# The last head pair's norm is taken up during the attention, through a buffer in DRAM, and its new sample state is formed among its value projections

## The chip, the cores and the metric

The kernel runs on one core of a Trainium2 chip. The metric is device time in microseconds (us) of one execution. The core has five engines, each with its own queue that it works through in order: PE (TensorE, matmuls), DVE (VectorE), ACT (ScalarE), POOL (GpSimd) and SP (SyncE, which issues nearly all DMAs). They wait for each other by semaphores.

## The reference

One inference step of one decoder layer: 1024 prompt tokens and 8 x 4 sample tokens, model width 1024. Two branches read the same normalised input: sparse attention (8 heads, 2 key heads, the 256 best keys of an indexer) and retention (8 heads of 64). What the change touches is the retention and its merge:

```python
def _head_norm(o):
    mu = jnp.mean(o, axis=-1, keepdims=True)
    var = jnp.mean(jnp.square(o - mu), axis=-1, keepdims=True)
    return (o - mu) * lax.rsqrt(var + EPS)

def step(S, inp):                       # in _retention, over chunks of 128
    qc, kc, vc = inp
    inter = jnp.einsum('bchk,bhkv->bchv', qc * dec_in[None, :, :, None], S)
    scores = jnp.einsum('bchk,bshk->bhcs', qc, kc) * dmat[None]
    intra = jnp.einsum('bhcs,bshv->bchv', scores, vc)
    S = S * dec_chunk[None, :, None, None] + jnp.einsum('bchk,bchv->bhkv', kc * dec_out[None, :, :, None], vc)
    return S, inter + intra
...
yb = jax.nn.silu(gb) * _head_norm(ob).reshape(B, T, D_B).astype(x.dtype)
y = jnp.einsum('bte,ed->btd', jnp.concatenate([ya, yb], axis=-1), w_out)
```

The retention also returns its final state for the prompt and, for the sample tokens, the state that starts from a given one (`state_ret`).

## The kernel before

The kernel goes through stages: input norm, scores of the indexer, bisections that find each row's 256th best score, the retention in four pairs of heads (0 to 3), the sparse attention in eight query blocks, the output projection with its norm, and the gated embedding. A scheduler orders the instructions of each engine ahead of time by a simulated timeline; at run time each engine keeps that order. Tiles of a pool with the same tag share buffers (`bufs`), and a new tile waits until the one whose buffer it takes has been read for the last time, also by a DMA that stores it.

**The retention** (L1440 to L1513). For each pair there is a query-and-key phase and a value phase. Each has eight blocks of 128 tokens, 24 matmuls of 128 x 256 each (`mm_a`, lines L276 to L278; results `pqk` and `pvg`), and one product for the sample rows (`mm_s`). In the query-and-key phase DVE and POOL rotate each block (`rope`). In the value phase ACT takes the values and the gates out of `pvg` (`take_vg`: values scaled into `vv`, gates by Silu into `sg`, ten buffers), `chunk_mm` forms the scores of the block, and the sum of the block goes from PSUM to `acc[:, tb, :]` by ACT (L1502). After the eighth block `ret_sample` does the same for the sample rows: outputs against the given states `s0`, and then the new state (`vm` on DVE, `dst` on PE, `sso` on DVE, store to `ret_state_sample`). Then `norm_gate` runs twice, for the eight prompt blocks (16 columns of statistics) and for the sample rows (2 columns): statistics and coefficients gy and gz on DVE with a root on ACT, scaling of `acc` on ACT (L1117) and DVE (L1119), product with the gates on POOL, for pair 3 on DVE (L1122), and a store to `yb_d` in DRAM (L1123). Between the blocks, `steps` moves generators on by a step: `bp` (prompt bisection) and `bss` (sample bisection, with a conditional part whose branch is at L976) in pair 0, `ss` (the sample attention's selection, mostly DVE) in pairs 1 to 3. What is left of `bss` is issued at the start of pair 1 with high priority, but an engine comes to the branch only where its order has it.

**The attention** (L1551 to L1635). At its start SP loads `toep` (1 MB) for the position bias. For each query block and each of two key heads (kv): `near` from `toep` and the mask on DVE, scores `sa` on PE, `L` with its row minimum `mn` on DVE (L1602), exponentials on ACT (L1605), transposes `ptp` and products `ob` on PE. Query blocks (`qas`) and gates (`gat`) come by SP's loads, two buffers each. Beside this the generator `sa` runs the sample attention: gathers on POOL (`kvs`, `kw`, L1170) and its own matmuls. The output projection then reads `yb_d`.

## Time and profile before

| | us |
|---|---|
| median of three runs | 1051.2 (1048.44 to 1052.79) |
| the profiled execution | 1050.72 |
| its span | 1048.9 |
| mean granted PE clock | 0.976 |
| pair 1: query-and-key phase, value phase start | 400.05, 433.35 |
| pair 2: query-and-key phase, value phase start | 471.03, 505.19 |
| pair 3: query-and-key phase, value phase start | 549.38, 586.84 |
| end of pair 3's last value projection | 623.0 |
| first load of the output projection | 790.78 |

The starts are those of the first 128 x 256 matmul of a phase in the timeline. Times in profile rows are us from the start of the span, durations of one instruction in ns where the row says "mean ns". PEclk is the share of the full clock that the throttle granted.

### The profile page before, as it was taken

The page shows a single profiled execution, that of the slowest core. Times are in us where ns is not written, and L with a number is a line of the kernel's source. Part 1 is how long each engine was busy: PE and PEld are TensorE (multiplying, and loading weights), DVE is VectorE, ACT ScalarE, POOL GpSimd, SP SyncE. Part 2 cuts the span into 40 slices and gives each one's busy share as a digit, 9 for nine tenths or more (in the row PEclk, how much of TensorE's full clock was granted, in tenths as well). Part 3 has the DMA queues.
Part 4 walks back from the last instruction along what each step waited for, and adds up shares of the span by engine and source line. Part 5 has one row for each costly group of instructions (what it writes and reads, how often), then busy time and mean ns, then how long its engine had stood idle before and what let it go on. Part 6 is the DMA issues. An engine that isn't in the chain of part 4 may idle for free.

```text
span 1048.9 us, 19845 instructions
## 1 busy us (share of the span) xinstructions
PE 991.8 (95%) x7375; PEld 838.2 (80%) x7375; DVE 681.4 (65%) x2022; ACT 503.1 (48%) x1090; POOL 320.8 (31%) x425
## 2 busy tenths in 40 slices
PE   4999998999999899999899995999999999999998
PEld 3999997766776898889788783666666999999998
DVE  6847668898492657969949937787763423873332
ACT  5545565885434487612342335656545523442211
POOL 4203223121301522705803512634330522332200
PEclk9999999999999999999899995999999999999999
DMA  8211235545443311311210724533211312432211
GB/s 291 71 61 51 96 97 190 186 148 177 130 161 115 76 33 43 81 45 47 64 54 21 190 65 128 162 78 109 73 56 48 118 42 81 148 116 87 83 41 38
DMA packets 98310, 102.25 MB, mean 97 GB/s; under 512 B 21346, under 2 KB 88386, under 8 KB 95906
## 3 DMA queue, kind: packets, MB, share of 16 engines
q1 hardware_dynamic: 92450, 74.74, 23.7%
q0 software_dynamic: 5760, 26.22, 8.0%
q8 instruction: 58, 0.95, 0.4%
q14 instruction: 42, 0.34, 0.1%
HBM read 79.25 MB, written 21.68 MB: 96 GB/s over the span
## 4 chain that ended last, share of the span: by engine, by line
PE 45%; DVE 6%; DMA 2%; issue 1%; POOL 1%; ACT 1%; SPq 0%; DVEq 0%; ACTq 0%; POOLq 0%
PE ob L1620 4%; PE ptp L1612 4%; PE pg L276 3%; PE pg L278 3%; PE pg L277 3%; PE po L276 3%; PE po L277 3%; PE po L278 2%; PE sa L1596 2%; PE pvg L276 2%; PE pvg L277 2%; PE pvg L278 2%; PE sa L1597 1%; PE pty L1667 1%; PE pqk L276 1%
## 5 line engine op out<-in xcount | busy, mean ns | idle before, releaser
L1170 POOL DMA_INDIRECT kvs<-in_cache_kv,idx x64 | 64.2, 1003 | 84.1 <-ACT pT L1617 49.1
L276 PE MATMUL pvg<-whi_vgb,xh 128*128 128x256 f32 x256 | 76.2, 298 | 3.0 <-ACT sg L1062 1.8
L276 PE MATMUL pqk<-whi_qkb,xh 128*128 128x256 f32 x256 | 75.0, 293 | 3.3 <-DVE rp L1049 3.3
L277 PE MATMUL pvg<-wlo_vgb,xh 128*128 128x256 f32 x256 | 75.6, 295 | 0.0
L278 PE MATMUL pvg<-whi_vgb,xl 128*128 128x256 f32 x256 | 75.1, 293 | 0.0
L277 PE MATMUL pqk<-wlo_qkb,xh 128*128 128x256 f32 x256 | 74.1, 290 | 0.0
L276 PE MATMUL po<-whi_o,yTh 128*128 128x256 f32 x256 | 73.1, 286 | 0.4 <-DVE yaT L1631 0.4
L278 PE MATMUL pqk<-whi_qkb,xl 128*128 128x256 f32 x256 | 73.2, 286 | 0.0
L278 PE MATMUL po<-whi_o,yTl 128*128 128x256 f32 x256 | 72.8, 285 | 0.0
L276 PE MATMUL pg<-whi_g,yTh 128*128 128x256 f32 x256 | 72.7, 284 | 0.0
L277 PE MATMUL po<-wlo_o,yTh 128*128 128x256 f32 x256 | 72.7, 284 | 0.0
L278 PE MATMUL pg<-whi_g,yTl 128*128 128x256 f32 x256 | 72.3, 283 | 0.0
L277 PE MATMUL pg<-wlo_g,yTh 128*128 128x256 f32 x256 | 72.2, 282 | 0.0
L1605 ACT ACTIVATE L<-L,mn 128x128 f32<-128x128 f32 (+7 forms) x64 | 49.6, 777 | 15.0 <-DVE mn L1602 14.6
L511 DVE SCALAR_TENSOR_TENSOR score<-r,wi,score 128x384 f32<-128x384 f32 (+5 forms) x42 | 41.0, 976 | 23.0 <-ACT r L507 21.7
L1805 DVE TENSOR_TENSOR sgm<-pu,sgm 128x256 f32<-128x256 f32 x32 | 13.6, 424 | 64.8 <-PE pu L278 61.1
L276 PEld LDWEIGHTS pvg<-whi_vgb,xh 128*128 128x128 f32 x256 | 49.8, 195 | 5.4 <-ACT sg L1062 2.2
L276 PEld LDWEIGHTS pqk<-whi_qkb,xh 128*128 128x128 f32 x256 | 49.0, 191 | 6.4 <-issue 5.5
L186 POOL TENSOR_TENSOR wlo_g<-wraw_g,whi_g 128x256 fp32r<-128x256 f32 x32 | 27.1, 881 | 87.8 <-ACT whi_g L185 87.7
L1051 POOL TENSOR_TENSOR qk<-rp,rp 128x128 f32<-128x128 f32 (+1 forms) x36 | 29.6, 821 | 78.7 <-DVE rp L1048 49.3
L507 ACT ACTIVATE r<-si 128x384 f32<-128x384 f32 (+5 forms) x48 | 36.3, 758 | 32.0 <-PE si L365 30.6
L278 PEld LDWEIGHTS pqk<-whi_qkb,xl 128*128 128x128 f32 x256 | 49.1, 192 | 2.4 <-issue 2.4
(545 smaller groups left out, 3317.9 us busy)
## 6 DMA issues: line engine op xcount, KB each, us to landing
wraw_qkb<-in_w_in SPq DMA_DIRECT2D x16, 256.0 KB, 4.1
wraw_vgb<-in_w_in SPq DMA_DIRECT2D x16, 256.0 KB, 3.8
wraw_o<-in_w_out SPq DMA_DIRECT2D x8, 512.0 KB, 5.6
qas<-qas_d SPq DMA_DIRECT2D x8, 512.0 KB, 5.1
xr<-in_x_prompt SPq DMA_DIRECT2D x8, 512.0 KB, 3.9
wraw_g<-in_w_ple_gate SPq DMA_DIRECT2D x8, 512.0 KB, 4.3
out_y_prompt<-sgm SPq DMA_DIRECT2D x32, 128.0 KB, 1.7
qas_d<-qst SPq DMA_DIRECT2D x8, 384.0 KB, 2.7
```

The lines of the kernel that those rows point to most:

```text
L186: nc.gpsimd.tensor_tensor(lo[:, k, :n], raw, hi[:, k, :n].bitcast(F32), op=ALU.subtract)
L276: nc.tensor.matmul(pt[:, :n], ah, hi[:, k, :n], start=(k == 0), stop=False)
L277: nc.tensor.matmul(pt[:, :n], ah, lo[:, k, :n], start=False, stop=False)
L278: nc.tensor.matmul(pt[:, :n], al, hi[:, k, :n], start=False, stop=(k == kc - 1))
L507: nc.scalar.activation(r[:, :n], s[:, :n], AF.Relu)
L511: nc.vector.scalar_tensor_tensor(sc, r[:, :n], wi[:, qb, h:h + 1], sc, op0=ALU.mult, op1=ALU.add)
L1051: nc.gpsimd.tensor_tensor(q4[:, :, 0, :], t1[:rows, :, 0, :], t2[:rows, :, 0, :], op=ALU.subtract)
L1170: return nc.gpsimd.indirect_dma_start(out=dst, out_offset=None, in_=kvflat, in_offset=bass.IndirectOffsetOnAxis(ap=idx, axis=0))
L1596: nc.tensor.matmul(s[:, :wc], qas[:, h, :], kah[kv][:, c:c + wc], start=True, stop=False)
L1605: behind[0] = nc.scalar.activation(L[:, :n], L[:, :n], AF.Exp, bias=least, scale=-1.0, accum_out=sm[:, i4:i4 + 1])
L1612: nc.tensor.transpose(tp[:, i4 * 128:i4 * 128 + 128], P[i4][:, kb * 128:kb * 128 + 128], ident)
L1620: nc.tensor.matmul(ob[64 * o:64 * o + 64, :256], vtok[:, kb, kv * 64:kv * 64 + 64], pT[:, o * 256:o * 256 + 256], start=(kb == 0), stop=(k ...
```

## The change

For pair 3, the sums and gates of each block are stored to a new DRAM buffer `yr_d` as soon as the block is done. `norm_gate` still forms the statistics, the inverse deviation and the shift (now in tiles `mv`, `rstd`, `shift` that outlive the retention), but scales nothing. A generator `ln` (`last_norm`) does that in the attention, one block at a time through one tile `dn`: load, two scalings on DVE, product on POOL, store to `yb_d`; a step of it stands after the scores and after the outputs of each kv from query block 1 on. For all pairs, gates lie beside the sums in one tile `ag` with one buffer, prompt and sample columns are normed as one set of 18, and the new sample state is a function of its own, `new_state`: after the norm for pairs 0 to 2, after the fourth value block for pair 3. Five tiles are placed first in their pool.

```diff
+    yr_d = dram.tile([128, 9, 2, 128], F32, name="yr_d")
...
+    first = {t: rt.tile(shape, F32, name=t, tag=t, bufs=n) for t, shape, n in (
+        ("vm", [128, 8, NS], 1), ("gv", [128, 18], 1), ("st", [128, 18, 6], 1), ("ag", [128, 9, 2, 128], 1), ("so", [128, 64], 2))}
...
-    def take_vg(src, rows, tb, hp, name):
+    def take_vg(src, rows, tb, hp, name, sg, tag="vv"):
...
-        sg = rt.tile([128, 128], F32, tag="sg", bufs=10, name=f"sg{name}")
...
         nc.scalar.activation(sg[:rows], src[:rows, 128:256], AF.Silu)
...
-    def norm_gate(acc, sgs, ntb, rows, tb0, hp):
+    mv, rstd, shift = (lp.tile([128, 18, 2], F32, name="bmv"), *(lp.tile([128, 18], F32, name=t) for t in ("gy", "gz")))
+    nc.gpsimd.memset(mv[:, 16:, :], 1.0)
+
+    def norm_gate(ag, hp):
+
+        acc = ag[:, :, 0, :]
...
+        if hp == 3:
+            return
+        for i, n in enumerate(rows):
+            a = acc[:n, i // 2, (i % 2) * 64:(i % 2) * 64 + 64]
             if i % 4 < 3:
-                nc.scalar.activation(a, a, AF.Identity, bias=z_[:, i:i + 1], scale=y_[:, i:i + 1])
+                nc.scalar.activation(a, a, AF.Identity, bias=z[:n, i:i + 1], scale=y[:n, i:i + 1])
             else:
...
+        for t in range(9):
+            n = rows[2 * t]
+            nc.gpsimd.tensor_tensor(acc[:n, t, :], acc[:n, t, :], ag[:n, t, 1, :], op=ALU.mult)
+        nc.sync.dma_start(yb_d[:, :8, hp, :], acc[:, :8, :])
+        nc.sync.dma_start(yb_d[:NS, 8, hp, :], acc[:NS, 8, :])
...
-        acc = rt.tile([128, 9, 128], F32, tag="acc", bufs=1, name=f"acc{hp}")
-        sgs = []
+        ag = rtile([128, 9, 2, 128], "ag", 1, f"ag{hp}")
...
-            nc.scalar.copy(acc[:, tb, :], o)
+            nc.scalar.copy(ag[:, tb, 0, :], o)
+            if tb == (3 if hp == 3 else 7):
+                vvs = sample_in(hp, sh, ag)
+                if hp == 3:
+                    new_state(hp, qks[8], vvs)
             if tb == 7:
-                sgS = ret_sample(hp, qks[8], sh, acc)
+                ret_sample(hp, qks[8], vvs, ag)
+            if hp == 3:
+                nc.sync.dma_start(yr_d[:, tb], ag[:, tb])
...
+        if hp == 3:
+            nc.sync.dma_start(yr_d[:NS, 8], ag[:NS, 8])
+        norm_gate(ag, hp)
+        if hp < 3:
+            new_state(hp, qks[8], vvs)
...
+    def last_norm():
+
+        for t in range(9):
+            n = 128 if t < 8 else NS
+            a = at.tile([128, 2, 128], F32, tag="dn", bufs=1, name="dn")
+            nc.sync.dma_start(a[:n], yr_d[:n, t])
+            yield
+            for j in range(2):
+                i, js = 2 * t + j, slice(j * 64, j * 64 + 64)
+                nc.vector.tensor_scalar(a[:n, 0, js], a[:n, 0, js], mv[:n, i, 0:1], rstd[:n, i:i + 1],
+                                        op0=ALU.subtract, op1=ALU.mult)
+            nc.gpsimd.tensor_tensor(a[:n, 0, :], a[:n, 0, :], a[:n, 1, :], op=ALU.mult)
+            nc.sync.dma_start(yb_d[:n, t, 3, :], a[:n, 0, :])
+            yield
+
+    ln = last_norm()
```

How this moves instructions, at three places. Rows give the line (of the kernel before or of the changed one; the changed one's lines are up to 30 higher), the operation, what it writes and reads, the size, and the semaphores it waits for.

First ACT in pair 1's value phase, around the branch of the sample selection. Before (`sg1_2` is the gate of pair 1's third block, `acc0` the sums of pair 0):

```order
L1117 ACTIVATE acc0_4193<-acc0_4193,gz_5003,gy_5002 32x64 [waits DVE_49] x2
L1060 ACTIVATE vv1_2_5656<-pvg_5609,cst_63 128x64 [waits PE_49]
L1060 ACTIVATE vv1_2_5656<-pvg_5609,cst_63 128x64
L1062 ACTIVATE sg1_2_5657<-pvg_5609 128x128 [waits Pool_49]
L976 UNCONDITIONAL_BRANCH
L1502 COPY acc1_5446<-ret_5522 128x128 [waits DMAHW2_49,DVE_49,DMAHW6_49,PE_49,Pool_49]
L1060 ACTIVATE vv1_3_5726<-pvg_5679,cst_63 128x64 x2
L1062 ACTIVATE sg1_3_5727<-pvg_5679 128x128
```

And now (`ag_3685` is pair 0's tile, `ag1_5424` pair 1's; `pvg_5449`, `pvg_5516` and `pvg_5585` are its first three blocks):

```order
L976 UNCONDITIONAL_BRANCH
L1068 ACTIVATE vv1_2_5632<-pvg_5585,cst_63 128x64 [waits PE_49]
L1068 ACTIVATE vv1_2_5632<-pvg_5585,cst_63 128x64
L1117 ACTIVATE ag_3685<-ag_3685,gz_3692,gy_3691 128x64 [waits DVE_49]
L1117 ACTIVATE ag_3685<-ag_3685,gz_3692,gy_3691 128x64 x11
L1117 ACTIVATE ag_3685<-ag_3685,gz_3692,gy_3691 32x64 x2
L1070 ACT_TABLE_LOAD [waits DMAHW5_49,DMAHW6_49,DVE_49]
L1070 ACTIVATE ag1_5424<-pvg_5449 128x128 [waits Pool_49]
L1506 COPY ag1_5424<-ret_5499 128x128
L1070 ACTIVATE ag1_5424<-pvg_5516 128x128
L1506 COPY ag1_5424<-ret_5567 128x128 [waits PE_49]
L1070 ACTIVATE ag1_5424<-pvg_5585 128x128
```

The prompt part of pair 0's norm stood among pair 1's rotations; it is now behind the branch, and the first gate of pair 1 is behind it and waits for two DMAs (the stores to `yb_d`). PE at the same place now, from the end of the third block (`pvg_5585`) to the start of the fourth (`pvg_5654`):

```order
L278 MATMUL pvg_5585<-whi_vgb1_5012,xl_72 128x256
L1086 MATMUL second_3702<-qkT_5639 128x128 [waits DVE_49]
L976 UNCONDITIONAL_BRANCH
L1502 MATMUL ret_5567<-sbd1_3680,qkT_5570 128x128 [waits DVE_49]
L1504 MATMUL ret_5567<-vv1_1_5563,sm_5572 128x64 x2
L1493 MATMUL ret_5636<-vv1_2_5632,qk1_2_5154 128x128 [waits Activation_49]
L1002 MATMUL stot_4699<-ssm_3792,groupr_3790 128x1 [waits DVE_49]
L1008 MATMUL tbc_4702<-cst_63,sbits_3788 128x32 [waits DVE_49]
L1008 MATMUL tbc_4705<-cst_63,ssm_3792 128x32 [waits DVE_49]
L276 MATMUL pvg_5654<-whi_vgb1_5012,xh_71 128x256 [waits PE_49,Activation_49]
```

Before, PE came to the branch in the fifth block (`pvg_5750`), and its matmuls went on behind it. They are the fourth block's now, and these stand behind the selection's broadcast (`tbc`).

Second, DVE from pair 3 into the attention. Before, the last rows ahead of the first `L`:

```order
L1583 TENSOR_TENSOR near_8009<-toep_7941,cst_63 128x4x128
...
L1150 TENSOR_TENSOR vm_7801<-vvs3_7766,cst_63 32x512 [waits PE_49]
...
L1156 TENSOR_TENSOR sso_7804<-dst_7797,s0_3680 64x512 [waits PE_49]
...
L1119 TENSOR_SCALAR acc3_7374<-acc3_7374,bmv_7814,gy_7848 128x64 x4
L1122 TENSOR_TENSOR acc3_7374<-acc3_7374,sg3_0_7415 128x128 [waits Activation_49]
...
L1122 TENSOR_TENSOR acc3_7374<-acc3_7374,sgs3_7767 32x128 [waits Activation_49]
L1602 ISA L_7960,mn_7961<-sa_7962,near_7957 128x128 [waits DVE_49,PE_49]
```

And now:

```order
L1612 TENSOR_TENSOR near_7886<-toep_7818,cst_63 128x4x128
L1099 BN_STATS bst_7737<-ag3_7298 128x6 [waits Activation_49]
...
L1149 TENSOR_TENSOR ag3_7298<-ret_7705,ag3_7298 32x128 [waits DMAHW5_49,DMAHW3_49,Activation_49]
...
L1102 TENSOR_TENSOR gv_7774<-bmv_3690,cst_63 128x18 [waits DVE_49]
L1106 RECIPROCAL gy_3691<-gy_3691 128x18 [waits Activation_49]
L1107 TENSOR_TENSOR gz_3692<-gy_3691 128x18 [waits DVE_49]
L1108 TENSOR_TENSOR gz_3692<-gz_3692,gv_7774 128x18 [waits DVE_49]
L1109 TENSOR_SCALAR gz_3692<-gz_3692 128x18 [waits DVE_49]
L1631 ISA L_7837,mn_7838<-sa_7839,near_7834 128x128 [waits PE_49]
```

The new state, the scalings and the products are gone from between `near` and the first `L`; statistics and coefficients stay.

Third, SP in the attention now (before, only loads of `qas`, `gat`, `gaT` and `gpost` stood here):

```order
L1522 DMA yr_d_3675<-ag3_7298 32x256 [waits DMAHW7_49,DVE_49]
L1585 DMA dn_7976<-yr_d_3675 128x256 [waits DMAHW0_49,PE_49]
L1558 DMA qas2_7939<-qas_d_103 128x8x128 [waits DMAHW1_49,PE_49]
L1592 DMA yb_d_3674<-dn_7976 128x128 [waits DMAHW2_49,DMAHW0_49,Pool_49]
L1585 DMA dn_8048<-yr_d_3675 128x256 [waits DMAHW3_49,DMAHW2_49]
L1592 DMA yb_d_3674<-dn_8048 128x128 [waits DMAHW4_49,DMAHW3_49,Pool_49]
L1558 DMA qas3_8083<-qas_d_103 128x8x128 [waits DMAHW5_49,PE_49]
L1585 DMA dn_8135<-yr_d_3675 128x256 [waits DMAHW6_49,DMAHW4_49]
L1608 DMA gat_8085<-ga_d_112 128x4x128 [waits DMAHW7_49,DVE_49]
L1592 DMA yb_d_3674<-dn_8135 128x128 [waits DMAHW6_49,Pool_49]
```

Stores that wait for POOL's product now stand between SP's loads.

More of the change, by code (lines that the diff above doesn't have):

```diff
@@ new lines, in tile_step @@
+    mv, rstd, shift = (lp.tile([128, 18, 2], F32, name="bmv"), *(lp.tile([128, 18], F32, name=t) for t in ("gy", "gz")))
+    nc.gpsimd.memset(mv[:, 16:, :], 1.0)
+    def norm_gate(ag, hp):
+        acc = ag[:, :, 0, :]
+        st = rtile([128, 18, 6], "st", 1, "bst")
+        rows = [128] * 16 + [NS] * 2
+        for i, n in enumerate(rows):
+            nc.vector.bn_stats(st[:n, i, :], acc[:n, i // 2, (i % 2) * 64:(i % 2) * 64 + 64])
+            nc.vector.bn_aggr(mv[:n, i, :], st[:n, i, :])
+        v, y, z = rtile([128, 18], "gv", 1, "gv"), rstd, shift
+        nc.vector.tensor_tensor(v.rearrange("p (t h) -> p t h", h=2),
+                                mv[:, :, 1].rearrange("p (t h) -> p t h", h=2),
+                                epsn[:, :, 2 * hp:2 * hp + 2], op=ALU.add)
+        nc.scalar.activation(y, v, AF.Sqrt)
+        nc.vector.reciprocal(y, y)
+        nc.vector.tensor_tensor(z, y, y, op=ALU.mult)
+        nc.vector.tensor_tensor(z, z, v, op=ALU.mult)
+        nc.vector.tensor_scalar(z, z, -0.5, 1.5, op0=ALU.mult, op1=ALU.add)
+        nc.vector.tensor_tensor(y, y, z, op=ALU.mult)
+        nc.vector.scalar_tensor_tensor(z, mv[:, :, 0], -1.0, y, op0=ALU.mult, op1=ALU.mult)
+        if hp == 3:
+            return
+        for i, n in enumerate(rows):
+            a = acc[:n, i // 2, (i % 2) * 64:(i % 2) * 64 + 64]
@@ L1116, in norm_gate @@
             if i % 4 < 3:
-                nc.scalar.activation(a, a, AF.Identity, bias=z_[:, i:i + 1], scale=y_[:, i:i + 1])
+                nc.scalar.activation(a, a, AF.Identity, bias=z[:n, i:i + 1], scale=y[:n, i:i + 1])
             else:
-                nc.vector.tensor_scalar(a, a, mv[:rows, i, 0:1], y_[:, i:i + 1],
-                                        op0=ALU.subtract, op1=ALU.mult)
-        for t in range(ntb):
-            (nc.vector if hp == 3 else nc.gpsimd).tensor_tensor(acc[:rows, t, :], acc[:rows, t, :], sgs[t][:rows], op=ALU.mult)
@@ L1123, in norm_gate @@
-        nc.sync.dma_start(yb_d[:rows, tb0:tb0 + ntb, hp, :], acc[:rows, :ntb, :])
+                nc.vector.tensor_scalar(a, a, mv[:n, i, 0:1], y[:n, i:i + 1], op0=ALU.subtract, op1=ALU.mult)
+        for t in range(9):
[3 more added lines that the diff above has]
+        nc.sync.dma_start(yb_d[:NS, 8, hp, :], acc[:NS, 8, :])
     smask = C("smask", 32)
@@ L1127, in tile_step, with sample_in @@
     qmask = C("qmask").rearrange("p (b t) -> p b t", b=8)
-    def ret_sample(hp, qk, sh, acc):
+    def sample_in(hp, sh, ag):
         for j in range(2):
@@ L1607, in tile_step @@
                 more(0.4 + n / 1200)
+            if qb:
+                step(ln)
             ob = bank("ob", "o")
@@ L1632, in tile_step @@
                                     ob[:, :256].rearrange("p (c q) -> p c q", c=2), gv, op=ALU.mult)
+            if qb:
+                step(ln)
+    for _ in ln:
+        pass
     for _ in sa:
         pass
-    gaT = at.tile([128, 4, NS], F32, name="gaT")
+    gaT = at.tile([128, 4, NS], F32, tag="dn", bufs=1, name="gaT")
     nc.sync.dma_start(gaT, ga_d[:, :, T:])
```

55 lines of the change are left out of this document (13 added, 42 removed).

## The prediction

> **What bounds the kernel now.** First the head of the profile's page, for the bound: which engine is busy, and how long.
>
> ```profile
> PE 991.8 (95%) x7375; PEld 838.2 (80%) x7375; DVE 681.4 (65%) x2022; ACT 503.1 (48%) x1090; POOL 320.8 (31%) x425
> ```
>
> Then the table of stretches, cut where the stages of the retention and of the attention begin: length, busy time of each engine (instructions), PE's granted clock.
>
> ```profile
> core 0: us, PE busy (x) PEld busy (x) DVE busy (x) ACT busy (x) POOL busy (x), PEclk, DMA share, GB/s
> 433.00:471.00 38.00, 35.52 (x296) 32.05 (x288) 27.38 (x91) 11.81 (x37) 13.39 (x25) 1.00 0.30 79
> 471.00:505.00 34.00, 34.00 (x286) 29.89 (x283) 31.71 (x80) 7.41 (x19) 20.93 (x21) 1.00 0.16 45
> 505.00:549.00 44.00, 40.03 (x295) 35.56 (x293) 29.73 (x95) 20.95 (x58) 16.86 (x24) 0.92 0.24 59
> 549.00:587.00 38.00, 36.78 (x331) 31.98 (x331) 35.62 (x136) 10.61 (x30) 15.37 (x26) 1.00 0.18 47
> 587.00:623.00 36.00, 34.83 (x280) 32.84 (x279) 20.91 (x92) 11.65 (x40) 10.01 (x18) 0.95 0.46 119
> 623.00:636.00 13.00, 8.79 (x68) 5.34 (x66) 8.45 (x36) 6.96 (x18) 5.70 (x8) 0.78 0.83 246
> 636.00:650.00 14.00, 5.56 (x17) 3.37 (x17) 9.75 (x45) 7.47 (x22) 0.00 (x0) 0.50 0.23 62
> 650.00:668.00 18.00, 16.48 (x104) 12.13 (x104) 14.12 (x58) 12.71 (x44) 12.82 (x13) 0.79 0.52 154
> 668.00:790.00 122.00, 121.98 (x912) 77.14 (x909) 89.79 (x325) 70.22 (x148) 49.06 (x50) 1.00 0.31 88
> ```
>
> PE is the bound: 95% busy, and full from 668 to 790. So an edit moves the end only where PE idles or runs at a low clock, or where it makes PE wait. Two places idle: 505 to 623 (value phase of pair 2, then pair 3), with 3.97 + 1.22 + 1.17 = 6.4 us idle and, at clocks 0.92 and 0.95, 44 x 0.08 + 36 x 0.05 = 5.3 us of lost speed; and 623 to 668, with 4.2 + 8.4 + 1.5 = 14.2 us idle at clocks of 0.5 to 0.8. The second is the hand-over from the last pair to the attention. Its chain of waits:
>
> ```profile
> 623.52 6.63 DMA toep<-toep_d
> 630.18 1.62 DVE near L1583 x2
> ...
> 632.28 0.35 DVE bst L1088 x2
> ...
> 633.27 1.98 PE dst L1152 x2
> ...
> 640.39 0.91 ACT acc L1117 x3
> 641.40 3.09 ACT acc L1117 x9
> ...
> 647.58 1.28 ACT L1605
> ```
>
> After `near` (done at 631.80) come the new sample state (two pairs of dst, at half clock), the norm of the prompt blocks (12 activations on ACT, 8 products on DVE), and the norm of the sample rows. Only then:
>
> ```profile
> 647.20 0.29 DVE L1602 CUSTOM_DVE_ANT_0 L<-sa,near 128x128 f32<-128x128 f32 x1
> PE sa L1596 <- DVE mn L1602: 8.1, 1, 8.1
> ```
>
> The first score block leaves PSUM at 647.20 (first row, from the timeline), 15.4 us after `near` could have let it, and PE waits 8.1 us for it (second row, from the waits of PE).
>
> **Part one, the hand-over: -12 us.** In the changed order of DVE, behind `near` stand 2 + 2 statistics (two took 0.35 us), their aggregates, three sums of 32 rows, gv, a trip to ACT for the root, and four small operations on 18 columns: some 16 operations at half of 0.35 us, 2.8, and the trip, which I put at four such, 0.7: 3.5 us. The two dst pairs, sso, the activations and the products are gone from there. The first L comes at about 631.8 + 3.5 = 635.3 in place of 647.20: 11.9 us earlier. What is late next is the toep load (6.63 us) with `near`, which stay. The new stores to yr_d are hidden: the last three blocks' stand behind the toep load on SP, and if they delayed it by their share (0.375 of its 1 MB), that would be 2.5 us. Bounds: 9, with that delay; 15, if PE also stays warmer (650 to 668 ran at 0.79, so 18 x 0.21 = 3.8 us could come back).
>
> **Part two, the new state among the value projections: +1 us.** The four dst matmuls, two vm and the sso operations move into pair 3's value phase. Their group:
>
> ```profile
> L1152 PE MATMUL dst<-vm,qk 32*64 32x512 f32 x16 | 10.3, 730 | 3.5 <-DVE vm L1150 3.5
> ```
>
> That group has all pairs; pair 3's four are at most 4 x 0.73 = 2.9 us of PE in a phase with 1.2 us idle; 0 if all of it falls into stalls. I take 1.
>
> **Part three, one buffer for sums and gates: +17 us, then -7.** The gates (Silu, L1062) had ten buffers of their own. The root and the small operations that the sample rows had for themselves are gone; they lie beside a full PE and cost and bring nothing. But the gates now share `ag`, which has one, so the first gate of pair 1 waits until pair 0's norm, its products on POOL and the store to yb_d are through. Pair 0's norm also moves: its 16 + 2 columns are one set, so it waits for the sample rows, and the order of ACT, DVE and POOL has it behind the branch of the sample selection (L976). PE has its three pvg banks full after the third block; the order has the fourth block's matmuls behind that. First today's rows from the timeline, then the prices from the groups and the DMA issues:
>
> ```profile
> 426.94 4.08 ACT L1117 ACTIVATE acc<-acc,gz,gy 128x64 f32<-128x64 f32 x12
> 445.95 0.37 PE L276 MATMUL pvg<-whi_vgb,xh 128*128 128x256 f32 x1
> 452.96 0.22 DVE L992 SCALAR_TENSOR_TENSOR ssm<-ssm 128x1 f32<-128x1 f32 x1 [3.13 <-DVEq L976]
> 461.91 0.16 DVE L1003 COPY ssm<-stot 128x1 f32<-128x1 f32 x1 [1.14 <-PE stot L1002]
> 463.73 0.32 SPq L1018 DMA_DIRECT2D mnew_d<-sjk  x1
> 467.32 0.58 SPq L1192 DMA_DIRECT2D X<-xs_d  x1
> L1122 POOL TENSOR_TENSOR acc<-acc,sg x24: 442/455/2540, 430.0 to 590.5; 128x128 f32<-128x128 f32 x24
> yb_d<-acc SPq DMA_DIRECT2D x4, 512.0 KB, 4.5
> L1062 ACT ACTIVATE sg<-pvg x32: 264/278/353, 371.3 to 623.4; 128x128 f32<-128x128 f32 x32
> L1062 ACT ACT_TABLE_LOAD  x4: 1283/1283/1283, 439.3 to 592.2; - x4
> ```
>
> Today the norm starts at 426.94, the fourth block at 445.95, and DVE leaves the branch at 452.96. In the change, from there: gz, gy, gz to about 454.7; 14 activations at 4.08 / 12 us to 459.6; the last product 0.46 later, with some queueing 460.7; the store, issue and 4.5 us, to 465; table load and gate 1.28 + 0.28: the fourth block starts near 466, 20 us late. A second wait guards it: the order puts that block behind the broadcast that follows 461.91, so even a quick store gives no start before 463.5. Against the 20: PE does the sums of two blocks (about 2 us) and today's own 2.5 us of idle in 433 to 471 falls into it; and it starts again at half clock, as at 636 to 650, for some 2 us. 20 - 2 - 2.5 + 2 is 17.5; I take 17, bounds 14 and 21.
>
> Behind the waiting gate on ACT stand the copies of pair 1's first three sums and the next blocks' scalings: PE waits for those through its banks, and DVE for the copies, for its statistics. On SP, behind the two stores to yb_d that wait for POOL (to 460.7), stand mnew_d and the loads of the selection (X). Today these are issued at 463.73 and 467.32, so they are not late.
>
> Part of the 17 comes back. The selection for the next pairs is DVE's, and its loads hang on that chain and not on PE, so it can start when it does today while PE is 17 us behind; the collisions that cost PE 6.4 + 5.3 = 11.7 us from 505 to 623 partly dissolve. They don't all: DVE has 31.7 of 34 us to do at 471 to 505, its order interleaves the selection with PE's blocks, and the smaller waits of the same kind in pairs 2 and 3 (their yb_d stores stand behind weight loads on SP) cost 1 to 3. I take -7, bounds 0 and -11.
>
> **Part four, the norm of the last pair in the attention: +2 us.** Nine loads, 18 DVE operations, nine POOL products, nine stores, two steps per kv from the second query block on; the prices from the groups and the DMA issues, then two issues from the timeline:
>
> ```profile
> L1119 DVE TENSOR_SCALAR acc<-acc,bmv,gy x16: 296/303/311, 424.9 to 640.9; 128x64 f32<-128x64 f32 x16
> L1170 POOL DMA_INDIRECT kvs<-in_cache_kv,idx x64 | 64.2, 1003 | 84.1 <-ACT pT L1617 49.1
> qas<-qas_d SPq DMA_DIRECT2D x8, 512.0 KB, 5.1
> 671.01 0.52 SPq L1545 DMA_DIRECT2D qas<-qas_d  x1
> 687.01 0.52 SPq L1545 DMA_DIRECT2D qas<-qas_d  x1
> ```
>
> DVE: 18 x 0.3 = 5.4 us, hidden in the 32 us that it has free from 668 to 790. POOL: 9 x 0.46 = 4.1 us in 73 free. The queue is the risk: the order of SP has query loads behind stores that wait for POOL. A query load is issued 16 us ahead (671.01, 687.01) and lands in 5.1, so a hold under 10.9 us costs nothing. That cover fails only if several gathers (about 1 us each) and a load stand in front of a product. Bounds 0 and 7; 2 is nearer to the covered case.
> [...]
>
> **The sum.** +17 - 7 + 1 - 12 + 2 = +1, against the profiled execution of 1050.72 (0.5 below the median of 1051.2): **1051.7 us**. Two large terms cancel, so the sign is open.
>
> **The rivals.**
> *Faster: the stall is absorbed.* The fourth block starts at its earliest (+14), all 11.7 us of collisions go (-11), the hand-over gives 13, the rest +1: 1050.7 - 9 = 1042. For it: 505 to 549 loses 7.5 us to waits on DVE, which would have been served already. Against: DVE was 93% busy from 471 to 505.
> *Slower: DVE can't run ahead.* In the new order DVE's statistics of pair 1's first blocks stand ahead of the first selection work, and they read sums that ACT copies behind the gate. If DVE halts there as long as PE, nothing dissolves: +18 + 0 + 1 - 12 + 2 = +9, 1060. It decides where the order has more than two of those statistics ahead of the selection.
> *Slower: SP's queue.* Holds over 10.9 us, in blocks where many gathers stand in front of a product on POOL: +7 in place of +2, and 1.5 for a restart at half clock: 1058.
> *The change doesn't do what it says.* If the first L waits for something else at the hand-over (the clock, the table load 1.28, the store of the last sums), only 5 of 12 come: +17 - 7 + 1 - 5 + 2 = +8, 1059.
>
> **How the numbers follow.** Forecast 0.40, absorbed 0.30, DVE can't run ahead 0.17, SP's queue 0.07, no shorter hand-over 0.06. The likeliest one's own range is 1046 to 1056. Since cases of both signs hold much, the range goes from 1039 (bounds 14, -11, 0, -15, 0: 1050.7 - 12) to 1063 (stall 21 and nothing back: 21 + 0 + 1 - 12 + 2). A measurement of this kernel can tell about 0.5% from no change: faster 0.30, same 0.40, slower 0.30.
>
> **What would show it.** Right: a gap of 15 us or more on PE between the third and fourth value block of pair 1, ended by ACT's gate, with ACT waiting for the store of pair 0; the first L 11 to 13 us after the last value projection; PE full from 668 on. Wrong: the fourth block before 460; idle and low clock from 505 to 623 unchanged; PE waits for qas; L later than 18 us after the last value projection.

## The result, and the profile after

| | before | the change |
|---|---|---|
| median of ten runs each, taken together, us | 1050.16 (1048.44 to 1052.79) | 1056.63 (1049.63 to 1060.77) |
| ratio to before | | 1.0052 (95% interval 1.0028 to 1.0076) |
| profiled execution, its span | 1050.72, 1048.9 | 1056.67, 1054.9 |
| mean granted PE clock | 0.976 | 0.974 |
| pair 1: value phase starts | 433.35 | 435.56 (+2.2) |
| pair 2: query-and-key phase starts | 471.03 | 486.96 (+15.9) |
| end of pair 3's last value projection | 622.99 | 631.83 (+8.8) |
| first score block on DVE | 647.20 | 644.73 (-2.5) |
| last of the 136 score operations on DVE | 790.79 | 795.92 (+5.1) |
| end of the span | 1048.9 | 1054.9 (+6.0) |

The change is slower by about half a per cent; the forecast was 1051.7 in a range of 1039 to 1063, so the measured time lies inside it. The differences in brackets are the reading: wherever one grows or shrinks from row to row, time was lost or won in that stage. They give +13.7 in pair 1's value phase, -7.1 over pairs 2 and 3, -11.3 at the hand-over, and +8.5 from the first score block to the end. Another 2.2 us stand there before any of it. The start of pair 0's value phase alone lies between 362.6 and 369.8 over the profiles of this study, so a difference of 2 us between two single profiles before the retention says nothing.

The page's head first, then the table of stretches of the changed kernel, cut at its own phases (columns as before: length, busy time of each engine, granted clock, DMA share, GB/s):

```profile
PE 990.3 (94%) x7375; PEld 838.7 (80%) x7375; DVE 671.8 (64%) x1991; ACT 496.0 (47%) x1070; POOL 316.8 (30%) x435
```

```profile
435.50:487.00 51.50, 42.22 (x297) 37.92 (x297) 37.11 (x112) 19.21 (x59) 14.38 (x25) 0.83 0.24 65
487.00:520.40 33.40, 33.27 (x279) 29.18 (x279) 31.67 (x95) 11.05 (x27) 18.11 (x26) 1.00 0.18 43
520.40:562.60 42.20, 39.06 (x330) 36.29 (x329) 23.60 (x108) 14.64 (x48) 12.63 (x21) 0.92 0.21 55
562.60:597.40 34.80, 34.80 (x308) 30.70 (x305) 28.91 (x113) 10.80 (x27) 20.95 (x37) 1.00 0.33 85
597.40:632.00 34.60, 34.60 (x274) 31.01 (x274) 13.79 (x55) 10.49 (x38) 1.55 (x4) 1.00 0.46 116
632.00:645.00 13.00, 7.30 (x68) 5.79 (x68) 8.90 (x42) 7.48 (x16) 5.71 (x8) 0.79 0.96 286
645.00:666.00 21.00, 17.46 (x104) 12.91 (x104) 14.12 (x61) 10.47 (x39) 14.07 (x14) 0.81 0.52 148
666.00:676.00 10.00, 7.68 (x46) 4.62 (x48) 6.17 (x26) 5.33 (x14) 2.71 (x4) 0.66 0.27 76
676.00:790.00 114.00, 113.27 (x847) 70.47 (x840) 83.78 (x306) 63.68 (x137) 48.86 (x53) 1.00 0.34 98
```

PE's busy time is nearly the same (990.3 against 991.8 us). Pair 1's value phase has 9.3 us idle and the clock falls to 0.83. Pair 3 now runs without idle time and at full clock (34.80 of 34.80, 34.60 of 34.60), which it did not before. In the attention the surprise is 666 to 676: 2.3 us idle and a clock of 0.66, where the kernel before was full from 668 on.

The stall of pair 1, from the timeline (start, duration, engine, line, operation; in brackets the idle time ahead and what ended it):

```profile
448.84 0.28 PE L278 MATMUL pvg<-whi_vgb,xl 128*128 128x256 f32 x1
451.21 0.22 DVE L992 SCALAR_TENSOR_TENSOR ssm<-ssm 128x1 f32<-128x1 f32 x1 [3.19 <-DVEq L976]
452.62 4.75 ACT L1117 ACTIVATE ag<-ag,gz,gy 128x64 f32<-128x64 f32 x14 [2.94 <-DVE gz L1111]
455.18 2.93 POOL L1122 TENSOR_TENSOR ag<-ag 128x128 f32<-128x128 f32 x7 [0.27 <-DVE ag L1119]
457.74 0.38 SPq L1123 DMA_DIRECT2D yb_d<-ag  x1
462.54 0.28 ACT L1070 ACTIVATE ag<-pvg 128x128 f32<-128x128 f32 x1
462.87 0.58 PE L276 MATMUL pvg<-whi_vgb,xh 128*128 128x256 f32 x1 [1.69 <-ACT ag L1070]
```

It is the predicted chain, link by link: branch, norm on ACT, product on POOL, store, gate, fourth block. The gap, here and below from the start of a block's last value matmul to the start of the next block's first, is 462.87 - 448.84 = 14.0 us; PE still does the sums of two blocks in it.

The hand-over, `near` and the first score block on DVE:

```profile
640.09 1.30 DVE L1612 TENSOR_TENSOR near<-toep,cst 128x512 f32<-128x512 f32 x2 [0.96 <-DMA toep<-toep_d]
644.73 0.29 DVE L1631 CUSTOM_DVE_ANT_0 L<-sa,near 128x128 f32<-128x128 f32 x1
```

`near` is done at 641.39, 9.6 us after the last value projection (8.8 before), and the score block follows 3.3 us later, in place of 15.4.

And the late norm in the attention, first DVE's rows, then SP's in the same stretch, then what SP and, from 650 to 720, PE waited for (engine, operation, releaser: total, times, longest):

```profile
652.61 0.42 DVE L1631 CUSTOM_DVE_ANT_0 L<-sa,near 128x256 f32<-128x256 f32 x1 [0.21 <-PE sa L1626]
656.27 0.54 DVE L1589 TENSOR_SCALAR dn<-dn,bmv,gy 128x64 f32<-128x64 f32 x2 [3.23 <-DMA dn<-yr_d]
656.72 0.42 DVE L1631 CUSTOM_DVE_ANT_0 L<-sa,near 128x256 f32<-128x256 f32 x1
...
666.27 0.54 DVE L1589 TENSOR_SCALAR dn<-dn,bmv,gy 128x64 f32<-128x64 f32 x2 [2.04 <-issue]
```

```profile
649.78 0.33 SPq L1592 DMA_DIRECT2D yb_d<-dn  x1
653.82 0.32 SPq L1585 DMA_DIRECT2D dn<-yr_d  x1
657.42 0.32 SPq L1592 DMA_DIRECT2D yb_d<-dn  x1
```

```profile
SPq L1585 <- DMA yb_d<-dn: 7.9, 4, 3.5
SPq L1558 <- PE sa L1626: 7.5, 2, 5.2
```

```profile
PE pkg L1355 <- ACT kgT L1356: 3.4, 1, 3.4
PE sa L1625 <- DVE mn L1631: 2.1, 2, 1.9
```

There is one tile `dn`, so a block's load (L1585) is issued only when the store of the block before it has landed: store at 649.78, load at 653.82. DVE comes to that block's scaling at 653, has nothing else that its order allows, and stands 3.23 us for the load; the next score block is behind it, at 656.72, and PE stands 1.9 us for that block. The query loads (L1558) wait for their own buffer, not for these stores. The 2.04 us of the last row have no named releaser ("issue": the profile shows nothing that the engine waited for), but SP's and POOL's waits on the same load's semaphore end at that moment too, at 666.2, 6.0 us after the load was issued at 660.20. The longest wait of PE, 3.4 us up to 668.32, is not for a score: it is for a copy of the sample attention on ACT (`kgT`), and what ACT waited for the profile does not name.

Three kernels below had one disturbed execution each (e2 2344.5 us, e7 1088.94, e10 3200.03), which the ratios leave out; e2's was the profiled one, so e2 has no phases.

### The profile page after: what moved, and what is told of

It is laid out like the page before. It is cut to its first block, busy times and chain, and to the rows that moved or that the text cites. A ratio compares the mean times of both kernels' runs of the same rounds, so it can differ in the third digit from the quotient of the medians.

```text
span 1054.9 us, 19856 instructions
## 1 busy us (share of the span) xinstructions
PE 990.3 (94%) x7375; PEld 838.7 (80%) x7375; DVE 671.8 (64%) x1991; ACT 496.0 (47%) x1070; POOL 316.8 (30%) x435
## 4 chain that ended last, share of the span: by engine, by line
PE 47%; DVE 4%; DMA 3%; ACT 1%; issue 1%; another core or an unknown queue 0%; SPq 0%; POOL 0%; ACTq 0%; DVEq 0%
PE ob L1651 4%; PE ptp L1643 3%; PE pg L276 3%; PE pg L278 3%; PE pg L277 3%; PE po L276 3%; PE po L277 3%; PE po L278 3%; PE pvg L276 2%; PE pvg L277 2%; PE pvg L278 2%; PE sa L1625 2%; PE sa L1626 1%; PE pqk L278 1%; PE pqk L276 1%
## 5 line engine op out<-in xcount | busy, mean ns | idle before, releaser
L1176 POOL DMA_INDIRECT kvs<-in_cache_kv,idx x64 | 64.5, 1008 | 108.4 <-ACT pT L1648 49.5
L277 PE MATMUL pqk<-wlo_qkb,xh 128*128 128x256 f32 x256 | 73.6, 287 | 0.0
L277 PEld LDWEIGHTS pvg<-wlo_vgb,xh 128*128 128x128 f32 x256 | 50.7, 198 | 1.3 <-issue 0.8
L278 PEld LDWEIGHTS pvg<-whi_vgb,xl 128*128 128x128 f32 x256 | 50.7, 198 | 0.7
```

What stands on the lines that cost most here:

```text
L277: nc.tensor.matmul(pt[:, :n], ah, lo[:, k, :n], start=False, stop=False)
L278: nc.tensor.matmul(pt[:, :n], al, hi[:, k, :n], start=False, stop=(k == kc - 1))
L1176: return nc.gpsimd.indirect_dma_start(out=dst, out_offset=None, in_=kvflat, in_offset=bass.IndirectOffsetOnAxis(ap=idx, axis=0))
```

## The experiments

The ratios below are to the kernel before in runs on the same chip; the medians come from several chips, so the ratios are what can be compared. Phase marks come from each run's profile. "First to last score" is the time from the first to the last of the 136 score operations on DVE: 143.6 us in the kernel before, 151.2 in the change.

| kernel | median, us | ratio (95%) | pair 2 starts | last value projection ends | to the first score | first to last score |
|---|---|---|---|---|---|---|
| before | | 1 | 471.0 | 623.0 | 24.2 | 143.6 |
| the change | 1056.63 | 1.0052 (1.0028 to 1.0076) | 487.0 | 631.8 | 12.9 | 151.2 |
| e1 split gates | 1064.5 | 1.0105 (1.0075 to 1.0136) | 480.5 | 636.1 | 13.7 | 154.3 |
| e2 gates apart | 1057.55 | 1.0043 (1.0008 to 1.0079) | | | | |
| e3 no late norm | 1050.19 | 0.9973 (0.9938 to 1.0008) | 485.6 | 629.3 | 13.0 | 145.3 |
| e4 norm from block 3 | 1053.94 | 1.0010 (0.9980 to 1.0041) | 485.9 | 630.6 | 13.1 | 150.6 |
| e5 norm pinned | 1049.91 | 1.0022 (1.0000 to 1.0044) | 491.1 | 636.1 | 13.4 | 143.5 |
| e6 product on DVE | 1052.73 | 1.0039 (1.0021 to 1.0057) | 489.6 | 633.7 | 13.1 | 148.3 |
| e7 two parts, pinned | 1043.82 | 0.9951 (0.9929 to 0.9973) | 470.1 | 623.0 | 12.5 | 145.1 |
| e8 state moved alone | 1049.28 | 1.0006 (0.9986 to 1.0025) | 468.9 | 621.6 | 18.6 | 146.4 |
| e9 two parts, not pinned | 1048.98 | 1.0006 (0.9984 to 1.0027) | 470.0 | 622.8 | 12.6 | 151.8 |
| e10 late norm alone, pinned | 1048.51 | 0.9997 (0.9970 to 1.0025) | 469.7 | 620.6 | 18.2 | 146.6 |
| e11 e7, weights on DVE | 1048.61 | 0.9999 (0.9979 to 1.0019) | 470.1 | 628.0 | 16.5 | 146.4 |
| e12 e1, weights on DVE | 1042.43 | 0.9956 (0.9933 to 0.9979) | 468.4 | 616.1 | 14.5 | 149.0 |

### The shared buffer: e1 and e2

e2 gives the gates nine buffers of their own again and leaves the norm of 18 columns. e1 also splits the norm of pairs 0 to 2 into 16 and 2 columns, as before.

```diff
+    def gate(name):
+        return rt.tile([128, 128], F32, tag="sg", bufs=9, name=name)
...
-            vv = take_vg(pt, 128, tb, hp, f"{hp}_{tb}", ag[:, tb, 1, :])
+            sgs.append(gate(f"sg{hp}_{tb}"))
+            vv = take_vg(pt, 128, tb, hp, f"{hp}_{tb}", sgs[tb])
...
-        norm_gate(acc, sgs + [sgS], hp)
+        for lo, hi in ((0, 16), (16, 18)) if hp < 3 else ((0, 18),):
+            norm_gate(acc, sgs + [sgS], hp, lo, hi)
```

(The last pair of lines is e1's alone.)

> The change with its part three undone: gates of all pairs in nine buffers of their own again, and the norm of pairs 0 to 2 in two sets again (16 prompt columns, then 2 sample columns). Theory (the 13.7 us between the third and fourth value block of pair 1 come from the merged norm and the shared buffer, and only part of it is won back later): no gap over 4 us there, last value projection ends at 623 to 626 in place of 631.9, attention unchanged, so 1047 to 1051 us. Rival (what is won back later is lost again when the stall goes): value phases end at 630 or later, 1054 to 1057 us.

> The change with only the gates in nine buffers of their own again; the norm stays one set of 18 columns. Theory (it is the merged norm, waiting for the sample rows, that puts pair 0's norm behind the branch; a gate buffer of its own only takes the store out of the wait): the fourth value block of pair 1 still starts after 460, 1054 to 1057 us. Rival (the shared buffer alone makes the stall): the gap goes, 1047 to 1051 us.

e2 came out near its theory (1057.55, where 1054 to 1057 was expected): gates of their own bring nothing while the norm is one set (ratios 1.0043 and 1.0052). Whether its fourth block still starts after 460, no profile shows. e1 was a miss. The gap in pair 1 did shrink, from 14.0 to 4.0 us, and pair 2 started 6.4 us earlier. But its value phase lost that again, as the rival had it (the last value projection ends at 636.1), though the time lies above the rival's range too. It lost it in two gaps of 4.9 us, and more. From e1's timeline, DVE's longest row in the first of them, then POOL's rows beside it:

```profile
523.09 3.57 DVE L1251 TENSOR_TENSOR sm<-sm 128x32 f32<-128x32 f32 x1
```

```profile
523.04 0.44 POOL L1060 TENSOR_TENSOR qk<-rp,rp 32x128 f32<-32x128 f32 x1 [0.22 <-DVE rp L1057]
523.45 0.44 POOL L1061 TENSOR_TENSOR qk<-rp,rp 32x128 f32<-32x128 f32 x1
523.86 2.75 POOL L186 TENSOR_TENSOR wlo_qkb<-wraw_qkb,whi_qkb 128x256 fp32r<-128x256 f32 x4
```

A DVE operation on 32 columns that takes 0.17 us in e12 takes 3.57 us here and ends (526.66) as POOL's run of six ends (526.61). That suggested a cause, which e11 and e12 test below.

### What the late norm costs, and why: e3 to e6, and e9

e3 leaves out the scaling and the gating of the last pair: its raw sums go straight to `yb_d`, so its output is not the layer's and only its time counts. e4 starts the late norm's steps with query block 3.

```diff
-                nc.sync.dma_start(yr_d[:, tb], ag[:, tb])
+                nc.sync.dma_start(yb_d[:, tb, 3, :], ag[:, tb, 0, :])
```

```diff
-            if qb:
+            if qb >= 3:
                 step(ln)
```

> The change without the scaling and gating of the last pair: its raw sums are stored straight to the place that the output projection reads, and nothing is loaded, scaled or stored in the attention. Theory (the 8.5 us that are lost between the first score block and 690 come from DVE's waits for the loads of the stored blocks): no wait of DVE or PE for them, 1047 to 1050 us. Rival (the sample attention's chain of gathers ends those waits, whatever the late norm does): at most 2 us better, 1054 to 1057 us.

> The change with the late norm's steps from query block 3 on in place of 1. Theory (its waits hurt where the blocks are short and the queues still fill): most of the 8.5 us come back, 1048 to 1051 us. Rival (every step costs its load's wait, wherever it stands): 1055 to 1058 us. Rival (gathers): as without the move, 1055 to 1057 us.

Without the late norm the ratio is 0.9973 instead of 1.0052, and it is 145.3 us from first to last score instead of 151.2. So most of the attention's loss, 5.9 of the 7.6 us, goes with the late norm. e4 (1053.94, between its theory's range and its rivals') told little: the step's place in the program moved, but the scheduler put the operations nearly where they had been (first and last at 645.2 and 710.2, against 646.4 and 711.9), and first to last score stayed at 150.6.

e5 therefore fixes the order itself. `issue_after` holds the two scalings of a block behind the last score operation traced before them, in DVE's own queue; loads, stores and products stay. e6 leaves the order and takes POOL out of the round from load to store.

```diff
+            with tc.issue_after(last_L[0]):
                 for j in range(2):
...
-                            nc.vector.tensor_tensor_reduce(L[:, x0:x1], s[:, x0 - c:x1 - c], add, 1.0, least,
-                                                           op0=ALU.add, op1=ALU.min, accum_out=mn[:, i:i + 1])
+                            last_L[0] = nc.vector.tensor_tensor_reduce(L[:, x0:x1], s[:, x0 - c:x1 - c], add, 1.0, least,
+                                                                       op0=ALU.add, op1=ALU.min, accum_out=mn[:, i:i + 1]).ins
```

```diff
-            nc.gpsimd.tensor_tensor(a[:n, 0, :], a[:n, 0, :], a[:n, 1, :], op=ALU.mult)
+            nc.vector.tensor_tensor(a[:n, 0, :], a[:n, 0, :], a[:n, 1, :], op=ALU.mult)
```

> The change, with one thing more: the two late-norm operations of a block are put behind the last score reduction of the head group in whose step they stand, in VectorE's order. Same loads, stores, products. Theory (VectorE stands at the late norm's loads, 4.3 us in 640 to 700, and the score blocks behind it start late): VectorE waits under 1 us for these loads, the lag of the score blocks behind the kernel before no longer grows between 665 and 700, and the time falls by 3 to 6 us from the change's 1056.6, to 1050.5 to 1053.5. Rival (the transfers on SP's queue and the product on POOL are what costs, not the order on VectorE): 1055 to 1058, the wait only changes its name.

> The change with the late norm's product by the gate on VectorE instead of POOL: nine operations more on VectorE, one engine fewer between load and store. Theory (VectorE's place is the price): VectorE still stands at the loads, and does nine products of some 0.2 us more, so 1056 to 1059. Rival (POOL, which also gathers the sample attention's rows, holds the product and with it the store and the next load): the round from load to next load, 10.5 us at 643.3 to 653.8 in the change, gets over 2 us shorter and the time falls to 1050 to 1054.

With the order fixed, first to last score takes 143.5 us: the 7.6 us are gone, with all of the work still done. Each such figure is one profile's, but the profiles fall into two groups. Without a late norm, or with a pinned one, it is 143.5 to 146.6 us (before, e3, e5, e7, e8, e10, e11); where the scheduler placed the late norm, it is 148.3 to 154.3 us (the change, e1, e4, e6, e9, e12). The stretches of e5 in its attention, the same instants as the last rows of the change above:

```profile
666.00:676.00 10.00, 8.93 (x73) 5.62 (x71) 6.74 (x34) 7.79 (x22) 7.80 (x9) 1.00 0.68 178
676.00:790.00 114.00, 112.45 (x843) 72.26 (x841) 86.44 (x315) 62.72 (x132) 50.23 (x53) 1.00 0.34 98
```

The clock in 666 to 676 is 1.00 instead of 0.66. The first score of e5 comes 4.7 us later; counted from it, the same ten microseconds have 0.6 us idle at 1.00 in e5 and 2.3 us at 0.66 in the change. One number of the expectation was wrong: DVE still stands 4.5 us at these loads (the change: 5.0), as this row of its waits says:

```profile
DVE dn L1590 <- DMA dn<-yr_d: 4.5, 4, 2.0
```

With the waits that have no named releaser it is 6.0 against 7.0 us. So the length of the waits alone is not the price. Their place differs: in the change the first one of over 1 us ends 11.5 us after the first score, and PE then stands 1.9 us for a score; in e5 it ends 19.6 us after it, and PE stands 0.4 us for one. Score operations are queued behind DVE's waits in e5 too, so that the place is what counts is the likely reading, not a proof. How the loss reaches PE is seen in part: from first to last score PE is idle for 6.9 us in the change and 3.7 in e5, half of the 6.9 in the one wait for the sample attention's copy, and its busy time is 144.3 against 139.8 us, at a clock of 0.95 against 0.97. The total of e5 fell less than its attention, since this profile lies 4.1 us behind the change's where pair 2 starts. The time bears the fall out only in part, as the intervals of e5 and the change overlap.

e6 is not settled. Its time, 1052.73, lies in its rival's range (1050 to 1054) and below its theory's, but the rival's sign did not come: the round from the first load to the second takes 11.0 us (645.34 to 656.31; the change 10.5), and DVE stands 10.4 us at the loads. First to last score is 148.3 us, 2.9 less than in the change, and the two intervals overlap. So POOL's part in the round may be a share of the price; that it is the larger one, this run doesn't support.

e9 repeats the test of the order on another base: it is e7 (below) without `issue_after`.

> The kernel with the two parts and without the shared buffer (1043.8, ratio 0.9951), but with the late norm where the scheduler puts it on VectorE, as in the change. Theory (VectorE standing at the late norm's loads is the price): between the first and the last score block it loses 4 to 8 us more than its pinned sibling (which lost 1.5 there against the kernel before), VectorE waits for these loads on 4 or more occasions, time 1047 to 1052. Rival (the order matters only beside the other parts of the change): within 2 us of the sibling, 1042 to 1046.

It gives the clearest answer of the study. In the source, e7 and e9 differ in nothing but where 18 operations may stand on DVE; up to the first score all their engines have one order, and behind it the scheduler's order of the others follows. Their first scores come at 635.50 and 635.35. Their ratios are 0.9951 (to 0.9973) and 1.0006 (from 0.9984), and 0.0055 of 1050 is 5.8 us. First to last score is 145.1 against 151.8 us. The same stretch of both, e7's first, and then DVE's waits for the loads over the whole attention, e7's first again:

```profile
636.00:656.00 20.00, 18.67 (x119) 13.69 (x120) 15.01 (x66) 13.16 (x45) 15.12 (x14) 0.79 0.54 158
```

```profile
636.00:656.00 20.00, 15.40 (x87) 11.36 (x86) 14.75 (x61) 9.67 (x36) 12.73 (x13) 0.71 0.49 140
```

```profile
DVE dn L1601 <- DMA dn<-yr_d: 4.5, 2, 2.3
DVE dn L1600 <- DMA dn<-yr_d: 10.3, 7, 3.1
```

PE is busy for 3.3 us less and at a lower clock (0.71 against 0.79) in that stretch of e9, and DVE stands seven times at the loads. PE waits 1.9 us for scores there, and not at all in that stretch of e7; its longest wait, 3.0 us up to 656.38, is again one of the sample attention, for a gathered block. POOL issues these gathers (64 with a mean of 1008 ns in the change's page), and the late norm's products stand among them. So the order of the 18 operations costs the time, but how much of it goes through the scores and how much through POOL and the sample attention is open.

### The parts of the hand-over, and a version that beats both: e7, e8 and e10

These start from the kernel before, with its gates in nine buffers instead of ten and its norm in two sets. e8 moves the new state behind the fourth value block of pair 3, e10 makes the norm of pair 3 late (pinned), e7 does both, with one buffer for `st` instead of two.

```diff
+            if tb == (3 if hp == 3 else 7):
+                vvs, sgS = sample_in(hp, sh)
+                if hp == 3:
+                    new_state(hp, qks[8], vvs)
```

```diff
+            if hp == 3:
+                nc.sync.dma_start(yr_d[:, tb, 0], acc[:, tb, :])
+                nc.sync.dma_start(yr_d[:, tb, 1], sg)
...
+        if hp == 3:
+            return
```

> The kernel before (gates in buffers of their own, nine of them, norm of pairs 0 to 2 in two sets, one buffer of statistics instead of two) with the moved new state and the late norm, the latter behind the score reductions on VectorE. Theory (the one buffer for sums and gates costs the stall of pair 1; the other parts give the short hand-over at a small price): no gap over 5 us in pair 1, pair 2's query and key projections start at 471 to 474, the last value projection ends at 622 to 626, first score block 11 to 14 us after it, end 1041 to 1047. Rival (the slow clock and idle time of pair 2 and 3 that the stall made good come back in other places, as in the change with separate gates and a split norm, 1064.5): last value projection ends after 630, time 1050 to 1058.

> The kernel before (nine gate buffers instead of ten) with the new sample state of the last pair computed after the fourth value block, the norm left as it was. Theory (the hand-over is shortened by the norm's tail that leaves it, the state's own operations lie beside other work either way): within 2 us of the kernel before, 1048.5 to 1052.5, first score block 22 to 25 us after the last value projection. Rival (the state's loads, matmuls and stores are what lengthens the hand-over): first score block 12 to 18 us after the last value projection and 1042 to 1047.

> The kernel before (nine gate buffers) with the late norm of the last pair alone, behind the score reductions; the new sample state stays at the hand-over. It completes the split of the hand-over: the state moved alone took 5.6 of the 24.2 us between the last value projection and the first score block, both together 11.7. Theory (two pieces in one row on VectorE, ACT and TensorE, so they add): first score block 17 to 19 us after the last value projection, last score block 4 to 7 us earlier than in the kernel before, time 1043 to 1047. Rival (the state's pair of matmuls and sums is what the end hangs on, the norm lies beside it): 22 us or more, 1048 to 1052.

The way from the last value projection to the first score is 24.2 us before, 18.6 with the state moved, 18.2 with the late norm, 12.5 with both: 5.6 and 6.0 come off, and together 11.7. The parts add. My theory for e8 (the norm's tail is all that counts) was wrong by its phases: 18.6 lies just above its rival's 12 to 18. Yet e8's time is that of the kernel before, as the theory had it: its profile lost 2.8 us between first and last score and 3.9 behind them, and no run shows why. e10's mark was right, its time was not (1048.51, where 1043 to 1047 was expected; its interval reaches from 0.9970 to 1.0025, so this one is not settled).

e7 is faster than both kernels: 1043.82 us, ratio 0.9951. It keeps the short hand-over and has no stall in pair 1 (pair 2 starts at 470.1), as its theory had it.

### POOL beside DVE in pair 2: e11 and e12

e7 still has a gap of 10.7 us at 510.9 in pair 2's value phase, and e1 lost there. Both show a small DVE operation on two operands that takes some 3 us beside POOL's weight subtractions (2.9 us in e7, 3.57 in e1), as does the kernel before (2.89 us for 128x16, from 515.21). e11 (on e7) and e12 (on e1) do these subtractions on DVE:

```diff
-                nc.gpsimd.tensor_tensor(lo[:, k, :n], raw, hi[:, k, :n].bitcast(F32), op=ALU.subtract)
+                (nc.vector if lazy and name[0] in "qv" else nc.gpsimd).tensor_tensor(lo[:, k, :n], raw, hi[:, k, :n].bitcast(F32), op=ALU.subtract)
```

> The two parts with the pinned late norm (1043.8), and the low halves of the retention's weights (64 subtractions of 128 x 256) formed on VectorE instead of POOL. In its sibling PE stands 10.7 us at 511 in pair 2's value phase, where VectorE's operations with two operands take 2.9 us beside four such subtractions in a row on POOL. Theory (POOL's rows shut VectorE out): the gap in pair 2's value phase falls below 5 us, the last value projection ends 3 to 8 us earlier than 623.0, time 1036 to 1041. Rival (VectorE is full there, 31.7 of 34 us, and the subtractions only load it more): gaps of the same size elsewhere, 1044 to 1052.

> The change with separate gates and a split norm (1064.5, where pair 1's stall fell from 14 to 4 us and pair 2's value phase lost the gain again), with the weights' low halves on VectorE as in the run before it. Theory (POOL's rows shutting VectorE out are what lost the gain): pair 2's value phase gets shorter than 45 us (it had 49.2 from its first to its last block) and the time falls to 1050 to 1057. Rival (the loss is VectorE's own load or order): still above 1060.

The two contradict each other. e12 gained some 16 us on e1 (1.0105 less 0.9956, of 1050), more than its theory had, and is as fast as e7; its pair 2 value phase went from 47.3 us between first and last matmul to 33.9, without a gap over 3 us. e11 lost 5 us on e7 (0.9999 less 0.9951; 1048.61, in its rival's range), and the gap is still there, 10.9 us at 513.0. In e11 POOL subtracts nothing there, and DVE is busy without a break. From its timeline, DVE, POOL and the longest idle time of PE in the gap:

```profile
514.71 2.40 DVE L1243 TENSOR_TENSOR_SCAN cx<-sel,cx 128x1056 f32<-128x1056 bf16 x1
...
519.80 0.46 DVE L1510 COPY sbd<-ret 64x64 f32<-64x64 f32 x2
```

```profile
514.75 2.99 POOL L1053 TENSOR_TENSOR qk<-rp,rp 32x128 f32<-32x128 f32 x1 [2.67 <-DVE rp L1050]
```

```profile
520.32 1.12 PE L1514 MATMUL ret<-vv,sm 128*128 128x64 f32 x4 [5.42 <-DVE sbd L1510]
```

PE waits 5.42 us for the copy of `sbd`, and that copy has a scan, four subtractions, a coefficient and four scalings ahead of it in DVE's order since 514.71. In e11 the longest part of the gap is thus DVE's order and load, not POOL's run. For e1, that POOL's runs lost the gain is not shown: the edit also made the scheduler set another order, and no run took the one without the other.

## Why the prediction was right or wrong

| step | predicted | measured |
|---|---|---|
| stall of pair 1 | +17 (14 to 21) | +13.7 |
| given back in pairs 2 and 3 | -7 (0 to -11) | -7.1, the new state included |
| new state among the value projections | +1 | inside the row above; +1.0 and +2.6 in siblings |
| hand-over | -12 (9 to 15) | -11.3 |
| late norm in the attention | +2 (0 to 7) | +8.5, of it 7.6 from first to last score |
| in no step | 0 | +2.2 |
| sum | +1 | +6.0 |

The sum was off by 5 us and the time, 1056.7, lies in the wide range, 0.7 above the 1046 to 1056 of the likeliest case. Part of this is luck: the late norm came 6.5 us dearer than predicted, and the stall, 3.3 us cheaper, hid half of that. Of the three signs of being right, the first score came where it was due (12.9 us, for 11 to 13), the gap was 14.0 us (for 15 or more), and PE was not full from 668 on.

**The stall** had the right links and was 3 us too long, just under its lower bound. The norm's activations began at 452.62 instead of the predicted 454.7 and the store was issued at 457.74 instead of 460.7; the fourth block started at 462.87, not near 466, and that though the value phase had begun 2.2 us later. The second guard (no start before 463.5) was 0.6 us too late as well. Behind the stall PE's granted clock was 0.50 from 462.87 to 467 and 0.54 from there to 469, some 3 us of lost speed (4.13 x 0.50 + 2 x 0.46), where 2 were predicted. e7 and e9, with two norm sets and gates apart, have no such stall; by e2's time, gates apart alone bring nothing, but no profile shows its stall.

**What comes back** was sized right to about 1 us, and its reason gets some support. From pair 2's start to the end of the last value projection the five profiles with the stall (the change, e3 to e6) take 143.7 to 145.0 us; the kernel before and e7 to e10 take 150.9 to 152.9. e1, whose stall is short, takes 155.5. With the weights' subtractions on DVE it is 158.0 (e11) and 147.7 (e12), without a stall in either, so this stretch does not go by the stall alone. Of the 7.1 us, 4.4 came in pair 3 (73.6 us before, 69.2 in the change); pair 2's value phase still has 3.1 us idle at a clock of 0.92. That DVE's selection ran ahead during the stall fits this, but no run isolated it.

**The new state** cost about what was predicted, 1 us or somewhat more: pair 3's value phase, first value matmul to the end of the last, takes 37.1 us in e8 against 36.1 before, and 37.8 in e7 against 35.2 in e10.

**The hand-over** was right as a whole, in its mark (first score 12.9 us after the last value projection) and in its mechanism (3.3 us from `near` to the first score, for 3.5), and e8 and e10 show that state and norm hold half of it each.

**The late norm in the attention is the step that failed.** The prediction priced DVE's 18 operations, called their 5.4 us "hidden in the 32 us that it has free", and named SP's queue as the risk. It looked for a query load that comes late and for a product that waits for gathers. Products did wait: the fourth block's began at 680.28, behind three gathers and 4.2 us after its scalings at 676.11. But no query load came late for it, and PE never waited for one. It left out that DVE keeps its order, so that an operation of 0.3 us which waits for a load holds whatever is queued behind it, score blocks among it (656.27 and 656.72 above), whatever free time DVE has. And it left out that with one tile `dn` a load waits for the store before it to land (649.78 to 653.82), so the data are late just where the scheduler had put the scalings early. e5, and e7 against e9, change nothing but that order in the source, and 7.7 and 6.7 us between first and last score go with it; in run time e7 and e9 are clearly apart, e5 and the change are not. By which waits of PE the time goes is shown only in part, as said above.

**SP's queue.** In its rows above SP itself stands 7.9 us for stores to land, and its order had a part in the loads' lateness: the third load, at 660.20, stood behind a query load that waited for its own buffer until 659.58. But no run shows the +7 for late query loads, the bound of this step and a term of the rival of that name. What the runs showed in its place are loads that were late for DVE, which stands 5.0 us at them from 640 to 720, or 7.0 with the wait that has no named releaser.

Of the rivals, "DVE can't run ahead" needed nothing to come back, and 7.1 us did. "SP's queue" came near by its time (1058), but not by its cause.

## What to carry to other kernels

Before calling an operation on an underused engine hidden, write down what it waits for and what stands behind it in that engine's order: here two scalings that take 0.54 us together stood 3.23 us for their load, and the score block behind them waited too. The load, work and store round through the single buffer `dn` had the store's landing in it (7.9 us of SP's waits in four rounds), so place the consumer behind the work that it must not hold, and check that the scheduler leaves it there. When a change bundles several edits, try them apart: here two of them, with the 18 operations pinned on DVE, are worth 5 us (e7), and without the pin nothing (e9), while the whole bundle lost 5.5. What each of the other pieces costs stays open, since taking the shared tile and the merged norm out of the bundle (e1) made it slower still.

## What the runs showed of the hardware

In e1 a DVE operation with two operands took twenty times what it took in e12: 3.57 us for 128x32 (0.17 us in e12), across six POOL instructions in a row, each of 0.44 to 0.69 us. It started at 523.09, the first of POOL's six at 523.04, and it ended as the last of them did (526.66 and 526.61). In the kernel before, one of 128x16 took 2.89 us from 515.21, with POOL busy from 515.00 to 518.91; the same operation of the other three pairs took 0.13 to 0.15 us.

It was seen the other way too: beside a DVE scan of 2.40 us a POOL operation of 32x128 took 2.99 us in e11 (0.44 us in e1). The scan started at 514.71, POOL's operation at 514.75. The kernel before has it as well: beside scans of 2.35 us from 503.90 and 2.40 us from 508.68, POOL operations of 128x128 took 2.58 us from 503.93 and 2.60 us from 508.73, where the median of their line is 0.46 us.

In each of these cases it was the operation that started later that took long, and in the first two it took as long as several instructions of the other engine, not as one. Why, no run shows.
